# A hybrid pooling and attention trunk: one weight scaling goes from the vector engine to GpSimd, and the vector part of one mixing stage is issued a projection tile later

## Chip, cores and metric

The kernel runs on one core of a Trainium2 chip. The metric is the device time of one execution in microseconds (us), lower is better. Engines are named as the profile names them: PE is the matrix engine, DVE the vector engine, ACT the scalar engine, POOL is GpSimd, SP the engine that issues most of the transfers.

## What is computed

Two layers (DEPTH = 2) of a decoder trunk on 16 meta tokens and 512 tokens with 1024 channels, all in float32:

```python
h = RMSNorm(x)
u_pool, z_pool, c_q, c_kv, k_rope, z_mla, g_pool, g_mla = split(h @ W_in)
y_pool = W_pool_up( PoolMix(u_pool) * silu(z_pool) )
y_mla  = W_mla_up( MLA(c_q, c_kv, k_rope) * silu(z_mla) )
x = x + W_out( sigmoid(g_pool) * y_pool + sigmoid(g_mla) * y_mla )
```

PoolMix works on four groups of 128 channels with windows w = 2, 4, 8 and 16. For each group it takes the mean of the last w tokens (of as many as there are, for the first ones), subtracts the token itself and multiplies the result by a 128x128 matrix. MLA is causal attention with 8 heads; all heads share the rotary part of the key, `k_rope`, which has 32 channels and comes straight out of the input projection.

## The kernel before

Channels lie on the 128 partitions and tokens along the free axis (T = 528 with the meta tokens). Every float32 matmul is done as three (`mm3`, lines 186 to 188): each operand is split into a high part, written by ACT, and a low part, high subtracted from the original, written by DVE, and high x high, high x low and low x high are summed in PSUM. For weights this is done in `wload`: a transfer into a `raw` buffer (three of them, line 115), ACT copies the high part (line 181), DVE subtracts (line 182). `whi` and `wlo` have three buffers each.

The main sequence is a list of projections, `plan`, walked by the generator `stream`: for each 128-wide output tile it loads weights (four chunks of 512 columns ahead), issues the matmuls and then the tile's evacuation out of PSUM (`evac`). The PSUM pool `mm` has four buffers of one bank; layer 0 computes all tokens in two halves of 264 columns and so takes two buffers for a tile, layer 1 computes 512 columns in one for most of them. Other work is put between by hand: `up(name)` walks the stream until that projection is done, then the work that stands after it is issued. Afterwards a list scheduler orders the instructions of each engine, and the engines run in that order, waiting on semaphores.

The order of the projections around the change is: cq0 to cq4, u0, k0, u1, kr, k1, u2, k2, u3, k3, v, zp0, zp1, y0, zp2, y1, zp3, y2, cq5, y3, qr0, qr1. Here:

- `u0` to `u3` are the four pooling groups, evacuated by DVE (line 477), multiplied by the norm factor `rinv`.
- `kr` is the shared rotary key. It isn't split: its weights (`wkr`, 128x256) are multiplied in place by the norm gain in `wload` (line 177) and used as float32 by narrow matmuls (line 416).
- `k0` to `k3` are the heads' keys, evacuated by DVE (line 560).
- `v` (`v_body`) computes values into `vt`: four token tiles and one for the meta tokens, each in a PSUM buffer, read out twice by ACT (line 583, high part) and twice by DVE (line 584, low part). The matmuls for the meta tokens read copies in `pa` (line 592).
- `zp0` to `zp3` are gates: DVE scales (line 486), ACT takes a tanh (line 488), DVE combines (line 489).
- `y0` to `y3` are the 128x128 group matmuls; they read `ys`, the split result of the mixing stages.

A mixing stage m, `mix(m)`, builds the windowed sum of `u` by m + 1 doubling additions on POOL (line 499, results in the `tmp` pool of three buffers), then DVE multiplies by 1/w and subtracts `u` (line 502), corrects the first 16 columns (lines 505 and 506, layer 0 only), and ACT and DVE split the result (lines 277 and 278). In `go`, `mix(2)` stands after `up("u3")` and `mix(3)` after `up("k3")`, so ahead of `v`.

Of the kernel before, what the change touches and what calls it, by code (L numbers as in the profile page):

```python
# [14 lines left out]
ALU = mybir.AluOpType  # L15
# [3 lines left out]
P = 128  # L19
# [3 lines left out]
NM = 16  # L23
T = SEQ + NM
HALF = T // 2
W = 528
WU = 544
# [19 lines left out]
C_MM, C_VBD, C_INVF, C_CNT = 356, 372, 380, 381  # L47
# [25 lines left out]
def trunk(ctx, tc, xT, pos, win, wkr, wqb, wkb, wvb, wgr, wpu, wmu, wout, gains, const, yT):  # L73
    nc = tc.nc
    pe, act, dve, gp, sp = nc.tensor, nc.scalar, nc.vector, nc.gpsimd, nc.sync
# [11 lines left out]
    def nm(s):  # L87
        uid[0] += 1
        return f"{s}_{uid[0]}"

    def slot(tag, dt=F32, bufs=1, w=W):
        return sl.tile([P, w], dt, tag=tag, name=nm(tag), bufs=bufs)

    def tmp(w=W):
        return tp.tile([P, w], F32, tag="tmp", name=nm("tmp"), bufs=3)
# [13 lines left out]
    cst = cp.tile([P, N_CONST], F32, name="cst")  # L109
# [4 lines left out]
    def fetch(src, n, raw, eng):  # L114
        eng.dma_start(raw[:, :n], src)
        return raw

    def rawt():
        return wp.tile([P, 512], F32, tag="raw", name=nm("raw"), bufs=3)
# [22 lines left out]
    def other_loads(made):  # L142
        for k, m in ((2, 0), (4, 1), (6, None)):
            ins = sp.dma_start(xb[:, k:k + 2, :T], xT[:, k:k + 2, :])
            behind(ins, made)
            if m is not None:
                raw = rawt()
                behind(sp.dma_start(raw, win[0, MT_CKV + m, :, 512:1024]), made)
                early.append(raw)
        behind(sp.dma_start(cst, const), made)  # L150
        behind(sp.dma_start(posb[:, :T], pos.partition_broadcast(P)), made)
        dve.tensor_copy(maskw[:, 512 - P:], cst[:, C_MASK:C_MASK + P])
        dve.tensor_copy(identr, ident)
# [17 lines left out]
    def wload(src, n, gain, spare):  # L171
        raw = early.pop(0) if early else fetch(src, n, rawt(), sp)
        loads[0] += 1
        pool, th, tl, nb = (tp, "th", "tl", 2) if loads[0] <= 2 or spare else (wp, "whi", "wlo", 3)
        if gain is not None:
            v = raw[:, :n].rearrange("p (k m) -> p k m", k=8)
            dve.tensor_mul(v, v, gain.unsqueeze(2).to_broadcast([P, 8, n // 8]))
            return raw, None
        hi = pool.tile([P, W if pool is tp else 512], F32R, tag=th, name=nm("whi"), bufs=nb)
        lo = pool.tile([P, W if pool is tp else 512], F32R, tag=tl, name=nm("wlo"), bufs=nb)  # L180
        act.activation(hi[:, :n], raw[:, :n], AF.Copy)  # L181
        dve.tensor_sub(lo[:, :n], raw[:, :n], hi[:, :n].bitcast(F32))  # L182
        return hi, lo
# [10 lines left out]
    def stream():  # L194
# [3 lines left out]
        def load(i):  # L198
            g_, c = flat[i]
            n = min(512, g_.width - c)  # L200
            return wload(g_.src[:, c:c + n], n, g_.gain, g_.spare)
# [37 lines left out]
    def step():  # L239
        c = next(main, None)  # L240
        if c is None:
            flush()
            return False
        clk[0] += c
        while pend and pend[0][0] <= clk[0]:
            pend.pop(0)[1]()
        return True
# [5 lines left out]
    def flush():  # L253
        while pend:
            pend.pop(0)[1]()

    def upto(name):
        while name not in done:
            if not step():
                break  # L260
# [10 lines left out]
    def fill_now(ns):  # L271
        end = clk[0] + ns
        while clk[0] < end and step():
            pass

    def split(hi, lo, src, a, b):
        act.activation(hi[:, a:b], src, AF.Copy)  # L277
        dve.tensor_sub(lo[:, a:b], src, hi[:, a:b].bitcast(F32))  # L278
# [14 lines left out]
    def tables():  # L293
        ang, k = tmp()[:, :T], tmp()[:, :T]
        dve.tensor_scalar(ang, posb[:, :T], float(NM), None, op0=ALU.add)
        dve.tensor_scalar(ang, ang, cst[:, C_INVF:C_INVF + 1], None, op0=ALU.mult)
        dve.tensor_scalar(k, ang, 1.0 / TWO_PI, MAGIC, op0=ALU.mult, op1=ALU.add)
        dve.tensor_scalar(k, k, -MAGIC, None, op0=ALU.add)
        for c in (PI_A, PI_B, PI_C):
            dve.scalar_tensor_tensor(out=ang, in0=k, scalar=-c, in1=ang, op0=ALU.mult, op1=ALU.add)  # L300
        dve.tensor_scalar(ang, ang, 3.1415925, -3.1415925, op0=ALU.min, op1=ALU.max)
        act.activation(tcos, ang, AF.Sin, scale=0.5)
        act.activation(tsin, ang, AF.Sin)
        dve.tensor_mul(tcos, tcos, tcos)
        dve.tensor_scalar(tcos, tcos, -2.0, 1.0, op0=ALU.mult, op1=ALU.add)
# [7 lines left out]
    class Layer:  # L313
# [175 lines left out]
                dve.scalar_tensor_tensor(out=d, in0=t[:, :b - a], scalar=1.0, in1=d, op0=ALU.add, op1=ALU.mult)  # L489
            return ev  # L490

        def mix(self, m):
            u, x0 = self.us[m], self.x0
            s = u
            for e in range(m + 1):
                w = 1 << e
                lo_ = 2 * w if not self.last else NM + 2 * w - 1
                n = tmp(WU)
                gp.tensor_tensor(out=n[:, lo_:WU], in0=s[:, lo_:WU], in1=s[:, lo_ - w:WU - w], op=ALU.add)
                s = n  # L500
            f = tmp()
            dve.scalar_tensor_tensor(out=f[:, x0:T], in0=s[:, NM + x0:WU], scalar=1.0 / (2 << m),
                                     in1=u[:, NM + x0:WU], op0=ALU.mult, op1=ALU.subtract)
            if not self.last:
                dve.tensor_mul(f[:, 0:NM], s[:, NM:2 * NM], cst[:, C_CNT + NM * m:C_CNT + NM * (m + 1)])
                dve.tensor_sub(f[:, 0:NM], f[:, 0:NM], u[:, NM:2 * NM])
            t = "tl" if m % 2 else "th"
            self.ys[m] = (slot(f"u{m}", F32R), tp.tile([P, W], F32R, tag=t, name=nm(t), bufs=2))
            split(*self.ys[m], f[:, x0:T], x0, T)
# [466 lines left out]
        def go(self, nxt):  # L976
            l = self.l
            up = lambda name: upto((l, name))
            if l == 0:
                for k in range(8):  # L980
                    if k in (0, 1, 3, 5):
                        step()
                    self.split_h(k)
                    if k == 0:
                        other_loads(first)
            up("ckv1")
            if l == 0:
                for k in range(8):
                    self.square_x(k)
            self.norm_sums()  # L990
            if l == 0:
                tables()
            up("u1")
            self.mix(0)
            self.mix(1)
            up("u3")
            self.mix(2)
            up("k3")
            self.mix(3)
            up("qr1")  # L1000
            for s, (a, b) in enumerate(FULL):
                a0 = max(a, self.x0)
                self.stat(self.acc[:, a0:b], a0, b, C_CQ, self.acc_last)
            up("qn3")
            self.qk_stats()
            fill_now(2600)
            kq = self.prep(0)
            fill_now(2600)
            due[0] = None
            prev = None  # L1010
            for h in range(H):
                kn_ = self.head(h, kq, prev)
                self.gap()
                if h + 1 < H:
                    kq = self.prep(h + 1)
                self.pv(prev, (2, 3))
                prev = kn_
                self.gap()
            fill_now(1300)
            self.pv(prev, (0, 1))  # L1020
            fill_now(2600)
            if not self.last:
                self.meta_queries()
            self.pv(prev, (2, 3))
            up("gm7")
            flush()
            if not self.last:
                for p in range(4):
                    self.meta_out(p)
            up("o7")  # L1030
            if nxt is not None:
                for k in range(8):
                    nxt.split_h(k)
# [77 lines left out]
```

## Time and profile before

| | |
|---|---|
| timed runs, us | 803.83, 804.71, 804.91 (median 804.71) |
| profiled execution, us | 803.88 |
| its span, us | 802.1 |
| mean granted PE clock over the span | 0.998 |
| PE busy, share of the span | 99% |
| DVE, ACT, POOL busy | 66%, 51%, 25% |
| line 177 on DVE | two executions, 0.42 us each |
| line 499 on POOL (window additions) | 20, of 1.05 to 1.61 us |
| line 502 on DVE | 8, of 0.68 to 0.71 us |

In a timeline row the first number is the start in us from the span's start, the second how long it took (of all of them together, where a row says x2 or more), then engine, source line, operation, the tiles out<-in and their shape. A bracket tells how long the engine had been idle before it and which engine's instruction ended that. In the list of waits a row says who waited for whom, the total in us, how often, and the longest.

### The profile page before, as it was taken

Reading aid. Unit: us, or ns where it says so; the run is one execution under the profiler, and the core shown is the slowest. Engines: PE = TensorE matmul, PEld = TensorE weight load, DVE = VectorE, ACT = ScalarE, POOL = GpSimd, SP = SyncE. Lnnn points to the kernel's source line nnn. Section 1 sums busy time; section 2 is a strip of 40 time slices with the busy share of each in tenths; the row PEclk is TensorE's granted clock in tenths of the full one; section 3 lists DMA queues with packets and bytes.
Section 4 is the critical chain, followed back from the end, with each engine's and each line's share of the span. In section 5 each row is a group of like instructions: output and inputs, shape, how many; then the busy total and the mean of one; then the engine's idle time right before and its main releaser. Section 6 shows DMA issues by size and latency. Waiting matters only on the chain.

```text
span 802.1 us, 14590 instructions
## 1 busy us (share of the span) xinstructions
PE 790.6 (99%) x5321; PEld 712.6 (89%) x5321; DVE 528.1 (66%) x1134; ACT 413.0 (51%) x935; POOL 196.8 (25%) x261
## 2 busy tenths in 40 slices
PE   8999899999999999999999999999999999999998
PEld 8898799999999999999998898877788888887887
DVE  5557867545779897576363469665467888664942
ACT  7455555644565665643354436546445666654421
POOL 1023512201433231133000126112024333410600
PEclk9999999999999999999999999999999999999999
DMA  6242223334223222234652332334253322222273
GB/s 239 67 106 87 67 77 95 106 94 135 82 91 96 73 73 67 77 96 120 187 153 85 76 116 80 93 92 119 80 154 99 100 74 78 75 72 78 92 223 105
DMA packets 51688, 81.80 MB, mean 102 GB/s; under 512 B 8208, under 2 KB 16784, under 8 KB 51616
## 3 DMA queue, kind: packets, MB, share of 16 engines
q1 hardware_dynamic: 51472, 80.61, 34.0%
q8 instruction: 42, 0.69, 0.4%
q14 instruction: 30, 0.25, 0.1%
q10 hardware_dynamic: 144, 0.26, 0.1%
HBM read 74.48 MB, written 4.24 MB: 98 GB/s over the span
## 4 chain that ended last, share of the span: by engine, by line
PE 90%; DMA 4%; DVE 3%; issue 1%; ACT 1%; POOL 1%; SPq 0%; DVEq 0%; ACTq 0%; POOLq 0%
PE mm L186 26%; PE mm L187 26%; PE mm L188 26%; PE mm L799 2%; PE S L187 2%; PE S L188 2%; PE S L186 1%; PE o L805 1%; PE o L804 1%; DMA raw<-win 1%; PE mm L355 1%; PE S L458 1%; DVE wlo L182 1%; DMA xb<-xT 1%; DMA bc<-kdr 1%
## 5 line engine op out<-in xcount | busy, mean ns | idle before, releaser
L186 PE MATMUL mm<-hh,whi 128*128 128x264 f32 (+2 forms) x1096 | 346.6, 318 | 2.5 <-DVE u L477 1.6
L187 PE MATMUL mm<-hl,whi 128*128 128x264 f32 (+2 forms) x1096 | 344.1, 315 | 0.0
L188 PE MATMUL mm<-hh,wlo 128*128 128x264 f32 (+2 forms) x1096 | 342.9, 315 | 0.0
L182 DVE TENSOR_TENSOR wlo<-raw,whi 128x512 fp32r<-128x512 f32 (+2 forms) x251 | 187.3, 750 | 121.0 <-ACT whi L181 117.5
L181 ACT ACTIVATE whi<-raw 128x512 fp32r<-128x512 f32 (+2 forms) x251 | 150.2, 602 | 190.2 <-PE mm L187 125.2
L186 PEld LDWEIGHTS mm<-hh,whi 128*128 128x128 f32 x1096 | 206.1, 189 | 15.9 <-issue 2.4
L187 PEld LDWEIGHTS mm<-hl,whi 128*128 128x128 f32 x1096 | 206.7, 189 | 12.2 <-issue 0.4
L188 PEld LDWEIGHTS mm<-hh,wlo 128*128 128x128 f32 x1096 | 205.7, 188 | 12.6 <-issue 0.4
L536 POOL TENSOR_TENSOR racc<-racc,tmp 128x264 f32<-128x264 f32 (+1 forms) x15 | 14.6, 973 | 186.7 <-ACT tmp L535 186.7
L705 POOL TENSOR_TENSOR tmp<-kp,bc 64x528 f32<-64x528 f32 x16 | 24.6, 1537 | 113.8 <-DMA bc<-kdr 78.6
L777 POOL TENSOR_TENSOR pm<-pa,rs 128x16 f32<-128x16 f32 x32 | 11.6, 361 | 145.4 <-DVE rs L772 145.4
L887 POOL TENSOR_TENSOR tmp<-tmp,xb 128x264 f32<-128x264 f32 (+1 forms) x24 | 27.0, 1149 | 58.5 <-DVE tmp L885 32.3
L733 DVE CUSTOM_DVE_ANT_0 S<-S,maskw,nqs 128x272 f32<-128x272 f32 (+4 forms) x80 | 38.4, 498 | 1.6 <-PE S L188 1.2
L740 ACT ACTIVATE cq<-S,bia 128x400 f32<-128x400 f32 (+2 forms) x48 | 24.6, 516 | 21.6 <-DVE bia L767 11.6
L186 PE MATMUL mm<-u,whi 128*128 128x264 f32 (+1 forms) x108 | 35.3, 327 | 0.0
L188 PE MATMUL mm<-u,wlo 128*128 128x264 f32 (+1 forms) x108 | 34.9, 323 | 0.0
L186 PE MATMUL mm<-cq,whi 128*128 128x264 f32 (+1 forms) x108 | 34.7, 322 | 0.0
L187 PE MATMUL mm<-cq,whi 128*128 128x264 f32 (+1 forms) x108 | 34.7, 322 | 0.0
L188 PE MATMUL mm<-cq,wlo 128*128 128x264 f32 (+1 forms) x108 | 34.6, 322 | 0.0
L278 DVE TENSOR_TENSOR tl<-mm,th 128x512 fp32r<-128x512 f32 (+1 forms) x64 | 29.3, 482 | 6.8 <-ACT th L277 5.8
L779 POOL TENSOR_TENSOR cq<-cq,rs 128x384 f32<-128x384 f32 (+1 forms) x32 | 32.8, 1025 | 0.0
L277 ACT ACTIVATE th<-mm 128x512 fp32r<-128x512 f32 (+1 forms) x64 | 25.4, 433 | 10.6 <-PE mm L799 10.4
(250 smaller groups left out, 1372.2 us busy)
## 6 DMA issues: line engine op xcount, KB each, us to landing
raw<-win SPq DMA_DIRECT2D x143, 256.0 KB, 2.6
raw<-wout SPq DMA_DIRECT2D x32, 256.0 KB, 3.3
bc<-kdr SPq DMA_DIRECT2D x16, 264.0 KB, 3.5
raw<-wpu SPq DMA_DIRECT2D x16, 256.0 KB, 2.7
raw<-wmu SPq DMA_DIRECT2D x16, 256.0 KB, 2.6
raw<-wqb SPq DMA_DIRECT2D x12, 256.0 KB, 2.6
tmp<-xT SPq DMA_DIRECT2D x16, 132.0 KB, 3.2
tmp<-scr SPq DMA_DIRECT2D x7, 256.0 KB, 3.5
```

The source lines that it names most:

```text
L181: act.activation(hi[:, :n], raw[:, :n], AF.Copy)
L182: dve.tensor_sub(lo[:, :n], raw[:, :n], hi[:, :n].bitcast(F32))
L186: pe.matmul(out, wh, xh, start=start, stop=False)
L187: pe.matmul(out, wh, xl, start=False, stop=False)
L188: newest[0] = pe.matmul(out, wl, xh, start=False, stop=stop)
L277: act.activation(hi[:, a:b], src, AF.Copy)
L278: dve.tensor_sub(lo[:, a:b], src, hi[:, a:b].bitcast(F32))
L705: gp.tensor_mul(kf[r0:r0 + 64, :], self.kp[r0:r0 + 64, :], bc[r0:r0 + 64, :])
L733: dve.tensor_tensor_reduce(out=sv, in0=sv, in1=mask, scale=nqs[:, i, h:h + 1], scalar=3e38, op0=ALU.add, op1=ALU.min, accum_out=bia[:, c:c ...
L740: act.activation(pv, sv, AF.Exp, scale=-1.0, bias=bia[:, i:i + 1], accum_out=rs[:, c:c + 1])
L779: gp.tensor_mul(pt[i][:, NM:], pt[i][:, NM:], rs[:, i:i + 1].to_broadcast([P, n - NM]))
L887: gp.tensor_add(t[:, :b - a], t[:, :b - a], self.am[m][:, a:b])
```

## The change

Two edits. In `wload`, the multiplication of the shared key's weights by the gain is issued on POOL instead of DVE. And `mix` is cut in two: `window(m)` holds the additions on POOL, `mix(m, s)` the rest. For m = 0, 1 and 2 they are issued together as before. For m = 3 the additions stay where they were, after `up("k3")`, and the rest is issued after `up("zp0")`. The last addition of m = 3 writes only the columns that are read later, and into the slot `q3` instead of a `tmp` buffer; `q3` is otherwise first used by `qr1`.

In the scheduled program the multiplication stands on POOL ahead of the first window addition in layer 0, and ahead of the last cq4 accumulation (line 536) in layer 1. DVE's instructions of the fourth stage (lines 502, 505, 506 and 278 of before) leave the stretch of line 584 and stand between zp0's line 489 and zp1's line 486. On PE the second group of meta token matmuls of `v` moves a few instructions forward among those of zp0; the rest of the engines' orders is the same but for a few neighbours.

```diff
@@ wload
         if gain is not None:
             v = raw[:, :n].rearrange("p (k m) -> p k m", k=8)
-            dve.tensor_mul(v, v, gain.unsqueeze(2).to_broadcast([P, 8, n // 8]))
+            gp.tensor_mul(v, v, gain.unsqueeze(2).to_broadcast([P, 8, n // 8]))
             return raw, None
@@ class Layer
-        def mix(self, m):
-            u, x0 = self.us[m], self.x0
-            s = u
+        def window(self, m):
+            s = self.us[m]
             for e in range(m + 1):
                 w = 1 << e
                 lo_ = 2 * w if not self.last else NM + 2 * w - 1
-                n = tmp(WU)
-                gp.tensor_tensor(out=n[:, lo_:WU], in0=s[:, lo_:WU], in1=s[:, lo_ - w:WU - w], op=ALU.add)
+                a, n = (lo_, tmp(WU)) if e < m or m < 3 else (NM + self.x0, None)
+                if n is None:
+                    n = slot("q3")
+                    gp.tensor_tensor(out=n[:, a - NM:T], in0=s[:, a:WU], in1=s[:, a - w:WU - w], op=ALU.add)
+                    return n
+                gp.tensor_tensor(out=n[:, a:WU], in0=s[:, a:WU], in1=s[:, a - w:WU - w], op=ALU.add)
                 s = n
+            return s[:, NM:WU]
+
+        def mix(self, m, s=None):
+            u, x0 = self.us[m], self.x0
+            s = self.window(m) if s is None else s
             f = tmp()
-            dve.scalar_tensor_tensor(out=f[:, x0:T], in0=s[:, NM + x0:WU], scalar=1.0 / (2 << m),
+            dve.scalar_tensor_tensor(out=f[:, x0:T], in0=s[:, x0:T], scalar=1.0 / (2 << m),
                                      in1=u[:, NM + x0:WU], op0=ALU.mult, op1=ALU.subtract)
             if not self.last:
-                dve.tensor_mul(f[:, 0:NM], s[:, NM:2 * NM], cst[:, C_CNT + NM * m:C_CNT + NM * (m + 1)])
+                dve.tensor_mul(f[:, 0:NM], s[:, 0:NM], cst[:, C_CNT + NM * m:C_CNT + NM * (m + 1)])
                 dve.tensor_sub(f[:, 0:NM], f[:, 0:NM], u[:, NM:2 * NM])
@@ go
             up("k3")
-            self.mix(3)
+            s = self.window(3)
+            up("zp0")
+            self.mix(3, s)
             up("qr1")
```

## The prediction

> **What bounds the kernel now.** I read the page first, then the waits of PE, then the timeline of each engine around those waits, then windows of the same stretches.
>
> ```profile
> span 802.1 us, 14590 instructions
> ...
> PE 790.6 (99%) x5321; PEld 712.6 (89%) x5321; DVE 528.1 (66%) x1134; ACT 413.0 (51%) x935; POOL 196.8 (25%) x261
> ```
>
> ```profile
> PE mm L186 <- DVE vt L584: 2.8, 1, 2.8
> PE mm L186 <- DVE u L477: 1.6, 1, 1.6
> ```
>
> PE is busy for 790.6 of 802.1 us. An edit on DVE or GpSimd (POOL in the profile) can only pay where PE waits for it, and the list of PE's waits (us in total, times, longest) is led by these two, each happening once in the whole run. Both lie in layer 0, and the two edits touch the neighbourhood of one each. The profiled execution took 803.88 us (span 802.1, so 1.8 around it); the median of the three timed runs is 804.71, 0.83 more, and they spread over 1.08 us. I make the sum against 803.88 and then move it to the median. A change of 0.2%, about what a measurement of this kernel can tell from none, is 1.6 us.
>
> **First edit: the scaling of the shared key's weights (L177) leaves DVE.** Timeline of DVE, ACT, PE and POOL around 60 us:
>
> ```profile
> 58.52 0.48 DVE L526 SCALAR_TENSOR_TENSOR cq<-mm,gn,cq 128x264 fp32r<-128x264 f32 x1
> 60.68 0.43 DVE L177 TENSOR_TENSOR raw<-raw,gn 128x256 f32<-128x256 f32 x1 [1.67 <-DMA raw<-wkr]
> 61.02 0.68 DVE L182 TENSOR_TENSOR wlo<-raw,whi 128x512 fp32r<-128x512 f32 x1
> 61.62 0.77 DVE L477 TENSOR_TENSOR u<-mm,rinv 128x264 f32<-128x264 f32 x2
> ...
> 59.39 1.14 ACT L181 ACTIVATE whi<-raw 128x512 fp32r<-128x512 f32 x2
> ...
> 62.19 0.36 PE L186 MATMUL mm<-hh,whi 128*128 128x264 f32 x1 [1.64 <-DVE u L477]
> ...
> 62.47 1.47 POOL L499 TENSOR_TENSOR tmp<-u 128x542 f32<-128x542 f32 x1 [2.14 <-DVE u L477]
> ...
> 97.96 0.63 ACT L181 ACTIVATE whi<-raw 128x512 fp32r<-128x512 f32 x1 [1.22 <-PE mm L188]
> ```
>
> DVE has nothing to do from 59.00 but stands before L177 until the wkr weights land. Behind it wait a weight split (L182) and the read of the first u tile out of PSUM (L477). PE needs that PSUM buffer for the next u tile. Without L177, L182 waits only for its high part: the first of the two L181 begins at 59.39 and takes 0.63, so it ends at 60.02 instead of L182's present start of 61.02. I take 60.04, an estimate that adds 0.02 for the signal. L182 and L477 keep their spacing, so everything behind moves by 61.02 - 60.04 = 0.98 us: L477 starts at 60.64 and PE at 62.19 - 0.98 = 61.21. Of the 1.64 us wait 0.66 stays. **Gain 0.98.** Bounds: 0, if something else holds DVE as long; 1.64, the whole wait.
>
> On POOL the operation is not in this trace. Nearest rows of the groups by shape, then the timeline where the result is used and the same place in layer 1, then a window of it (columns: stretch, its length, busy us of PE, PEld, DVE, ACT and POOL, granted clock of PE, DMA share, GB/s):
>
> ```profile
> L779 POOL TENSOR_TENSOR pa<-pa,rs 128x256 f32<-128x256 f32 x16 | 10.6, 662 | 0.0
> L536 POOL TENSOR_TENSOR racc<-racc,tmp 128x264 f32<-128x264 f32 x10 | 8.1, 815 | 74.7 <-ACT tmp L535 74.7
> ```
>
> ```profile
> 68.21 1.99 PE L416 MATMUL mm<-xb,raw 128*32 128x264 f32 x32
> ...
> 463.02 1.29 POOL L536 TENSOR_TENSOR racc<-racc,tmp 128x512 f32<-128x512 f32 x1 [4.74 <-ACT tmp L535]
> ...
> 465.19 0.42 DVE L177 TENSOR_TENSOR raw<-raw,gn 128x256 f32<-128x256 f32 x1 [3.00 <-DMA raw<-wkr]
> ...
> 466.98 1.44 POOL L499 TENSOR_TENSOR tmp<-u 128x527 f32<-128x527 f32 x1 [2.67 <-DVE u L477]
> ```
>
> ```profile
> 462.00:512.00 50.00, 50.00 (x356) 44.39 (x355) 37.06 (x74) 27.70 (x61) 22.48 (x25) 1.00 0.31 92
> ```
>
> L779 multiplies in place by a broadcast operand over 128x256, as L177 does, in 0.66 us; L536 takes 0.82. I take 0.7: from about 60.68, when DVE's L177 shows the weights there, to 61.38. Its reader, the shared key's matmul L416, starts at 68.21 (67.23 after the move), so 5.9 us cover it. POOL's next work, the first window addition, can start at 62.47 - 0.98 = 61.49, after L177 is done. One transfer behind it on SP that reuses the same raw buffer gains a wait for POOL, but it waits for L416 already.
>
> In layer 1, L177 stands on POOL ahead of the last L536, which then slips from 463.02 to about 465.9 and ends near 467.2, 0.2 us after the addition L499 could have started. Nothing comes of it, nor of DVE's 3.00 us: PE is busy for 50.00 of the 50 us from 462 on. **Layer 1: 0.**
>
> A rule speaks against moving the multiply. Rows first (timeline, then windows of the same stretch): while POOL added, a 128x512 L182 took 1.51 us instead of 0.68, and a 16-wide L506 1.05.
>
> ```profile
> 90.28 1.51 DVE L182 TENSOR_TENSOR wlo<-raw,whi 128x512 fp32r<-128x512 f32 x1
> 91.72 1.05 DVE L506 TENSOR_TENSOR tmp<-tmp,u 128x16 f32<-128x16 f32 x1
> 93.48 1.21 DVE L278 TENSOR_TENSOR th<-tmp,u 128x528 fp32r<-128x528 f32 x1 [0.71 <-ACT u L277]
> 94.61 1.65 DVE L584 SCALAR_TENSOR_TENSOR vt<-mm,ny,vt 128x256 fp32r<-128x256 f32 x4
> 96.18 0.69 DVE L502 SCALAR_TENSOR_TENSOR tmp<-tmp,u 128x528 f32<-128x528 f32 x1
> ...
> 97.98 0.16 DVE L505 TENSOR_TENSOR tmp<-tmp,cst 128x16 f32<-128x16 f32 x1
> ...
> 99.23 0.17 DVE L506 TENSOR_TENSOR tmp<-tmp,u 128x16 f32<-128x16 f32 x1
> ...
> 100.16 0.71 DVE L278 TENSOR_TENSOR tl<-tmp,u 128x528 fp32r<-128x528 f32 x1 [0.37 <-ACT u L277]
> ...
> 90.16 3.97 POOL L499 TENSOR_TENSOR tmp<-tmp 128x540 f32<-128x540 f32 x3 [1.12 <-DVE tmp L505]
> ...
> 96.41 0.66 PE L186 MATMUL mm<-whi,pa 128*128 128x512 f32 x1 [2.80 <-DVE vt L584]
> ```
>
> ```profile
> 62.20:65.00 2.80, 2.80 (x23) 2.80 (x24) 2.14 (x6) 1.13 (x4) 1.47 (x1) 1.00 0.50 139
> ...
> 93.60:96.40 2.80, 0.00 (x1) 0.03 (x1) 2.80 (x6) 2.21 (x7) 0.53 (x1) 1.00 0.09 33
> 96.40:99.80 3.40, 3.40 (x13) 3.07 (x14) 3.18 (x10) 1.64 (x4) 0.00 (x0) 0.52 0.02 5
> ```
>
> The Trainium skill (SBUF — State Buffer, on the shared port pair) calls this an exclusive lock between GpSimd and a DVE operation with two SBUF inputs: who starts first has it for the whole instruction. The trace agrees in size. By that rule, were L177 first, L182 would wait out its 0.7 us and the gain would be 0.3. I expect DVE first: L182 can start at 60.04 and the weights come at 60.68.
>
> **Second edit: the fourth mixing stage.** PE's other wait, 2.80 us at 96.41, is for the PSUM buffer that the fourth L584 reads out. In DVE's queue that L584 stands behind a split, an L506 and an L278, all stretched by POOL's three additions of 90.16 to 94.13. The last addition now writes slot q3; it is the same addition at the same place. The DVE part that moves (L502, L505, L506 and the low half of its split, with the ACT half between) begins at 96.18, behind the fourth L584. So taking it away frees 0.69 us only after PE has been released. **The 2.80 us stay**, and with them their tail: the windows show the clock at 0.52 for 3.40 us right behind the gap, 3.40 x 0.48 = 1.63 us lost. All links of this chain hang on PE's earlier progress, so the whole stretch only shifts by the 0.98. From 99.80 on PE has no wait that the moved work could have caused: **gain 0**.
>
> What it may cost where it arrives, behind zp0's matmuls:
>
> ```profile
> 106.22 1.35 POOL L607 CAST vb<-tmp 32x128 fp32r<-32x128 f32 x4
> ...
> 107.88 0.43 DVE L489 SCALAR_TENSOR_TENSOR xb<-tmp,xb 128x264 f32<-128x264 f32 x1 [1.45 <-ACT tmp L488]
> ...
> 108.34 0.42 ACT L488 ACTIVATE tmp<-xb 128x264 f32<-128x264 f32 x1 [0.50 <-DVE xb L489]
> ...
> 108.80 0.43 DVE L489 SCALAR_TENSOR_TENSOR xb<-tmp,xb 128x264 f32<-128x264 f32 x1 [0.49 <-ACT tmp L488]
> 109.32 0.69 DVE L182 TENSOR_TENSOR wlo<-raw,whi 128x512 fp32r<-128x512 f32 x1
> 109.93 0.42 DVE L486 SCALAR_TENSOR_TENSOR xb<-mm,rinv 128x264 f32<-128x264 f32 x1
> ...
> 111.31 0.43 DVE L486 SCALAR_TENSOR_TENSOR xb<-mm,rinv 128x264 f32<-128x264 f32 x1
> ...
> 111.83 0.28 PE L186 MATMUL mm<-hh,whi 128*128 128x264 f32 x1
> ```
>
> In these times (all 0.98 earlier after): the new queue is L489, the subtraction, L489, two 16-wide operations, L182, the low half, then L486, which frees zp1's first PSUM buffer. The subtraction (0.69) fits between the L489s, which end at 109.27. The 16-wide ones bring DVE to 109.57, L182 to 110.2. Meanwhile ACT does the high half, 109.62 to 110.27 (0.65, an estimate from L181's 0.63 over 512 columns). The low half takes DVE to about 111.0, and L486 ends near 111.4 instead of 110.35. PE wants that buffer for zp2 at 111.83: 0.4 us of cover left. The second L486 still ends at its 111.74. So 0, with this small cover. In layer 1 the same insertion meets a DVE that is busy 37.06 of 50.00 us: 0.
>
> **Sum.** 803.88 - 0.98 = 802.90 in the profiled execution's terms; against the median 804.71 - 0.98 = 803.73, which I round to 803.7.
>
> **The rivals.**
> - The tail goes, the gap stays. The slow stretch is 3.40 us long, and 1.64 us of waiting at 62.19 drew none (clock 1.00 in the row of 62.20). So the clock may be judged in stretches of this length: the gap of 2.80 us, moved by 0.98, would then fall across two of them, neither idle enough. Gain 0.98 + 1.63 = 2.61: 802.1 against the median. Against: nothing ties such stretches to the kernel's start, so the gap may have fallen badly or well before too. Chance 0.18. The Trainium skill (TensorE: Matmul & The Clock Gate, Part 1) has such a window, about 3.4 us and free-running, which must be idle to halve the clock; the 3.40 us of the trace agree with its length.
> - The second gap goes too. For: DVE is busy all 2.80 us of it. A shift of 0.12 us would let the split at 90.28 go ahead of the addition at 90.16, and the queue behind would be shorter. Against: the same instructions stand ahead of the fourth L584. Gain 0.98 + 2.80 + 1.63 = 5.41: 799.3. Chance 0.18.
> - L177 was not the gate (gain 0), or POOL begins it before L182 and holds L182 up for its 0.7 us, as an addition held the one at 90.28 (gain 0.98 - 0.7 = 0.3): 804.4 to 804.7. The first needs a second hold on DVE of the same length, the second the weights 0.64 us earlier. Chance 0.08.
> - Slower: the inserted work makes zp1's evacuation late. Its operations in series (rows of 96.18 to 100.16) are 0.69 + 0.16 + 0.17 + 0.65 + 0.71 = 2.4 us. If nothing overlaps (POOL's L607 late for the subtraction's buffer, ACT late with the high half), L486 ends at 110.35 + 2.4 = 112.75 and PE, due at 111.83, waits 0.92 us plus 0.15 for the signal (the fourth L584 ends at 96.26, PE starts at 96.41). With a slow-clock tail of 1.63 that is 2.7 - 0.98 = +1.7: 806.4. It decides from 0.4 us of delay on, and is over 0.2% only with all of it and the tail. For: the cover is thin. Against: POOL's L607 ends at 107.57, before the subtraction can start. Chance 0.14.
>
> **How the numbers follow.** Forecast 0.42. Within 0.2% are the forecast and the third rival, 0.50; faster by over 0.2% the first two, 0.36; slower 0.14. The range reaches down to the second rival, 799.0, and up to 805.6, which covers the third with the spread of the runs upward (0.9); only the slower case is outside. The forecast's own range is 802.6 to 804.9.
>
> **What would show it.** Right: PE's wait for L477 near 0.66 us, L177 on POOL at about 0.7 us, the wait for L584 still about 2.8 us, and no wait of PE at the start of zp2. Wrong: the L584 wait below 2 us, the first wait unchanged, or a new wait of PE for L486.

## The result, and the profile after

| | before | after |
|---|---|---|
| runs of one comparison, median us | 804.81 (803.32 to 807.46, 20 runs) | 802.7 (800.62 to 805.44, 20 runs) |
| ratio, 95% interval | | 0.9972 [0.9963, 0.998] |
| profiled execution / span, us | 803.88 / 802.1 | 802.87 / 801.1 |
| mean granted clock in it | 0.998 | 1.0 |

Faster by 2.1 us, and by the whole interval faster than the kernel before: twice the 0.98 us forecast, in the forecast's direction and inside its range. Line numbers: `wload` is unmoved; the window additions (L499) are now L502, the last one L500; L502 of before is L510, and what follows is 8 higher as well (L506 is L514, L536 is L544, L584 is L592).

The page of after, its first rows:

```profile
span 801.1 us, 14595 instructions
...
PE 791.3 (99%) x5321; PEld 713.3 (89%) x5321; DVE 528.3 (66%) x1132; ACT 413.6 (52%) x935; POOL 199.2 (25%) x263
```

Nothing shows here but that POOL has two operations more and DVE two fewer. The list of PE's waits of after says where to look (us in total, times, longest):

```profile
PE mm L186 <- DVE vt L592: 2.8, 1, 2.8
...
PE mm L186 <- DVE u L477: 0.8, 1, 0.8
```

The wait for the first u tile fell from 1.6 to 0.8 us, the wait for vt is the same 2.8. The first of these can't be read as the gain by itself: before, run again below, waits only 0.8 us there too. The timeline of after around the first (DVE, ACT, PE, then POOL):

```profile
61.37 0.83 DVE L182 TENSOR_TENSOR wlo<-raw,whi 128x512 fp32r<-128x512 f32 x1 [1.04 <-ACT whi L181]
62.12 0.76 DVE L477 TENSOR_TENSOR u<-mm,rinv 128x264 f32<-128x264 f32 x2
...
60.72 1.14 ACT L181 ACTIVATE whi<-raw 128x512 fp32r<-128x512 f32 x2
...
62.69 0.36 PE L186 MATMUL mm<-hh,whi 128*128 128x264 f32 x1 [0.82 <-DVE u L477]
...
60.16 1.49 POOL L544 TENSOR_TENSOR racc<-racc,tmp 128x264 f32<-128x264 f32 x2 [3.75 <-ACT tmp L543]
62.16 0.62 POOL L177 TENSOR_TENSOR raw<-raw,gn 128x256 f32<-128x256 f32 x1 [0.51 <-DMA raw<-wkr]
62.96 1.47 POOL L502 TENSOR_TENSOR tmp<-u 128x542 f32<-128x542 f32 x1 [0.18 <-DVE u L477]
```

In this execution everything here begins later than in before's (the pair of L181 at 60.72 instead of 59.39), so compare from L181 on: L182 now waits for ACT's L181 and not behind a wait for a transfer, and PE restarts (its first matmul behind the wait) 62.69 - 60.72 = 1.97 us after L181's start, where it took 62.19 - 59.39 = 2.80. That is 0.83 us less. L177 takes 0.62 us on POOL, after DVE's L182 has begun.

The second place, DVE, PE and POOL of after:

```profile
90.79 1.51 DVE L182 TENSOR_TENSOR wlo<-raw,whi 128x512 fp32r<-128x512 f32 x1
92.22 1.05 DVE L514 TENSOR_TENSOR tmp<-tmp,u 128x16 f32<-128x16 f32 x1
93.98 1.21 DVE L278 TENSOR_TENSOR th<-tmp,u 128x528 fp32r<-128x528 f32 x1 [0.71 <-ACT u L277]
95.11 2.82 DVE L592 SCALAR_TENSOR_TENSOR vt<-mm,ny,vt 128x256 fp32r<-128x256 f32 x7
...
96.91 0.47 PE L186 MATMUL mm<-whi,pa 128*128 128x512 f32 x1 [2.81 <-DVE vt L592]
...
90.67 2.58 POOL L502 TENSOR_TENSOR tmp<-tmp 128x540 f32<-128x540 f32 x2 [1.12 <-DVE tmp L513]
93.32 1.31 POOL L500 TENSOR_TENSOR q<-tmp 128x528 f32<-128x528 f32 x1
```

The same three operations with the same durations to the hundredth (1.51, 1.05, 1.21) as before, beside the same additions. What differs is behind the gap: windows of after, two of 3.4 us around PE's restart and two longer ones (length, busy us of PE, PEld, DVE, ACT and POOL, granted clock, DMA share, GB/s).

```profile
93.50:96.90 3.40, 0.59 (x3) 0.18 (x2) 2.92 (x6) 2.82 (x8) 1.13 (x1) 1.00 0.22 74
96.90:100.30 3.40, 3.39 (x25) 3.26 (x26) 2.39 (x7) 1.34 (x3) 0.00 (x0) 1.00 0.02 6
...
105.00:112.00 7.00, 7.00 (x60) 7.00 (x59) 5.22 (x13) 4.98 (x11) 1.35 (x5) 1.00 0.21 64
...
462.00:512.00 50.00, 50.00 (x352) 44.18 (x352) 38.64 (x74) 27.78 (x61) 23.46 (x26) 1.00 0.28 85
```

The clock stays at 1.00 behind the gap, where before's profile had 0.52 for 3.40 us: no tail in this execution. PE is busy throughout from 105 to 112, where the moved DVE part arrives, and from 462 to 512, where layer 1 has its L177.

So after's profile has PE's restart 0.83 us earlier behind L181, the gap as it was, no tail. Is the missing tail the change's doing, and what would remove the gap? The experiments ask that.

### The profile page after: what moved, and what is told of

Same layout as the page of the kernel before. It is cut to its first block, busy times and chain, and to the rows that moved or that the text cites. A ratio compares the mean times of both kernels' runs of the same rounds, so it can differ in the third digit from the quotient of the medians.

```text
span 801.1 us, 14595 instructions
## 1 busy us (share of the span) xinstructions
PE 791.3 (99%) x5321; PEld 713.3 (89%) x5321; DVE 528.3 (66%) x1132; ACT 413.6 (52%) x935; POOL 199.2 (25%) x263
## 4 chain that ended last, share of the span: by engine, by line
PE 90%; DVE 3%; DMA 3%; issue 1%; ACT 1%; POOL 1%; SPq 0%; ACTq 0%; DVEq 0%; POOLq 0%
PE mm L186 26%; PE mm L188 26%; PE mm L187 26%; PE mm L807 2%; DMA raw<-win 2%; PE S L187 2%; PE S L188 2%; PE S L186 2%; PE o L813 1%; PE o L812 1%; PE mm L355 1%; DVE wlo L182 1%; PE S L458 1%; DMA bc<-kdr 1%; PE mm L416 0%
## 5 line engine op out<-in xcount | busy, mean ns | idle before, releaser
L182 DVE TENSOR_TENSOR wlo<-raw,whi 128x512 fp32r<-128x512 f32 (+2 forms) x251 | 186.6, 747 | 121.9 <-ACT whi L181 115.2
L181 ACT ACTIVATE whi<-raw 128x512 fp32r<-128x512 f32 (+2 forms) x251 | 150.2, 602 | 186.8 <-PE mm L187 136.7
L544 POOL TENSOR_TENSOR racc<-racc,tmp 128x264 f32<-128x264 f32 (+1 forms) x15 | 14.9, 996 | 182.4 <-ACT tmp L543 158.5
```

## The experiments

Theories, as the expectations use the letters: **A**, only the first edit makes a lasting gain, by what DVE stood in front of L177, and the rest of the 2.1 us is how often the slow clock follows the gap. **B**, the second edit brings that rest, by making the slow clock rarer. **C**, the two edits pay only together. Beside them stands the question what makes the gap: the additions, as the prediction has it, or something else. Each ratio is against the runs of the kernel before in the same comparison.

### Each edit alone, and both kernels again

The first edit alone is before with one line changed:

```diff
-            dve.tensor_mul(v, v, gain.unsqueeze(2).to_broadcast([P, 8, n // 8]))
+            gp.tensor_mul(v, v, gain.unsqueeze(2).to_broadcast([P, 8, n // 8]))
```

> Only the first edit: L177 on POOL, the fourth mixing stage as before. Theory A (the first edit is the whole lasting gain, about 1 us; the rest of the 2.1 us is how often the slow clock follows the 2.8 us gap): 1.0 us under before in the mean, PE's wait for the first u tile 0.6 to 0.9 us, the wait for L584 2.8 us, and the slow clock in some executions only. Theory B (the second edit brings the missing 1.1 us, by making the slow clock rarer): also 1.0 us under before, but the slow clock about as often as before. Theory C (the two edits only work together): less than 0.5 us.

Measured: 801.51 us (12 runs), ratio 0.9989 [0.9979, 0.9998], against 802.52 (35 runs) of before. Its timeline, DVE, ACT, PE, POOL:

```profile
60.03 0.84 DVE L182 TENSOR_TENSOR wlo<-raw,whi 128x512 fp32r<-128x512 f32 x1 [1.04 <-ACT whi L181]
60.79 0.76 DVE L477 TENSOR_TENSOR u<-mm,rinv 128x264 f32<-128x264 f32 x2
...
59.37 1.14 ACT L181 ACTIVATE whi<-raw 128x512 fp32r<-128x512 f32 x2
...
61.35 0.36 PE L186 MATMUL mm<-hh,whi 128*128 128x264 f32 x1 [0.45 <-DVE u L477]
...
58.82 1.50 POOL L536 TENSOR_TENSOR racc<-racc,tmp 128x264 f32<-128x264 f32 x2 [3.75 <-ACT tmp L535]
```

This execution begins the stretch at the same moment as before's profile did (L181 at 59.37 and 59.39), so the absolute times can be compared: L182 starts at 60.03 (predicted 60.04), L477 at 60.79 instead of 61.62, PE at 61.35 instead of 62.19. It gains 0.84 us, not 0.98, because L182 takes 0.84 here and 0.68 in before. Here it begins while POOL's pair of L536 (58.82 to 60.32) is still running, in before it began after it. PE's wait is 0.45 us, under the 0.6 to 0.9 expected, because PE comes to it later than in before's profile: 61.35 - 0.45 - 59.37 = 1.53 us after L181's start, where it was 62.19 - 1.64 - 59.39 = 1.16. The wait for vt is 2.8 us.

The second edit alone is after with `dve` in that line:

> Only the second edit: L177 stays on DVE. Theory A: 0 +- 0.4 us against before, both of PE's waits as before (1.6 and 2.8 us). Theory B: 1.1 us under before, and the granted clock is 1.000 in more executions than before. Theory C: less than 0.5 us.

Measured: 802.07 (11 runs), ratio 0.9994 [0.9986, 1.0003]; the wait for vt 2.8 us, the first wait 1.1 where 1.6 was expected. It can't be told from before.

After again:

> The changed kernel once more, on the same chip as its two halves. Theory A: 1 to 2 us under before, the mean clock below 1.000 in about half of the executions, as in the 20 of the first comparison. Theory B: 2.1 us, and e1 and e2 add up to it.

Measured: 800.79 (12 runs), ratio 0.998 [0.9972, 0.9989]; the wait for vt 2.8 us.

Before again, as a measure of what a comparison can tell:

> The kernel before against itself, for its spread and for how often its clock is below 1.000. Theory A: about as often as in the changed kernel (half), and a difference of 0 +- 0.4 us. Theory B: clearly more often than in the changed kernel.

Measured: 802.07 (11 runs), ratio 0.9993 [0.9982, 1.0004]. The same kernel comes out 0.45 us under its own median, so half a microsecond is not a difference here. The two edits alone, 0.9989 and 0.9994, multiply to 0.9983, beside 0.998 for both: nothing needs theory C.

Before's second profile also shows how PE's first wait varies (DVE, ACT, PE):

```profile
59.65 0.42 DVE L177 TENSOR_TENSOR raw<-raw,gn 128x256 f32<-128x256 f32 x1 [1.77 <-DMA raw<-wkr]
...
58.26 1.21 ACT L181 ACTIVATE whi<-raw 128x512 fp32r<-128x512 f32 x2
...
61.17 0.36 PE L186 MATMUL mm<-hh,whi 128*128 128x264 f32 x1 [0.82 <-DVE u L477]
```

With L177 on DVE, PE waits only 0.82 us here, because it comes to the wait 61.17 - 0.82 - 58.26 = 2.09 us after L181's start. From L181 to PE's restart it is 2.91 us, no shorter than the 2.80 of the first profile. So the gain of the first edit is read from that stretch and not from the wait.

Executions that list a mean clock of 0.999 or more are taken here as those without the tail: the three profiles with one (before, after again, the second edit alone) list 0.997 or 0.998, the others 1.0. In this comparison they are 7 of 35 and 5 of 11 for before, 5 of 12 for the first edit alone, 4 of 11 for the second alone, 6 of 12 for both. The second edit alone has no more of them than before again, and the same median (802.07), not 1.1 us less: nothing speaks for B.

The profiles of after again and before again also answer for the tail. Windows of after again, then of before again, each with the 3.4 us up to the restart or the slow stretch and the 3.4 us behind:

```profile
92.40:95.80 3.40, 0.87 (x4) 0.77 (x5) 3.40 (x8) 2.28 (x6) 0.24 (x1) 1.00 0.01 2
95.80:99.20 3.40, 3.40 (x18) 3.40 (x17) 1.51 (x5) 0.99 (x2) 0.00 (x0) 0.51 0.09 24
```

```profile
91.90:95.30 3.40, 0.69 (x3) 0.21 (x2) 2.86 (x6) 2.82 (x8) 1.19 (x1) 1.00 0.19 72
95.30:98.70 3.40, 3.26 (x22) 2.83 (x23) 3.15 (x10) 2.06 (x5) 0.00 (x0) 1.00 0.02 5
```

After has the tail in this execution (0.51 for 3.4 us) and before has none: the reverse of the first two profiles, from the same two kernels. The tail comes in some executions of either kernel. It isn't something that the second edit takes away.

### The additions of the fourth stage moved too

In the next kernel both halves of the stage stand behind zp0's matmuls:

```diff
-            s = self.window(3)
             up("zp0")
-            self.mix(3, s)
+            self.mix(3)
```

> The changed kernel, but the additions of the fourth mixing stage move along with its DVE part, behind zp0's matmuls, so that no addition of GpSimd runs beside the split, the 16-wide operation and the subtraction that stand ahead of the fourth read of vt. Theory (the wait of 2.8 us is made by those three, stretched by GpSimd's three additions): they take 0.68 + 0.17 + 0.71 again instead of 1.51 + 1.05 + 1.21 us, so the wait falls by about 2.2 to about 0.6 us, and without a gap of that length no stretch at half clock follows it: nearly every execution at full clock, the median 2.2 + 0.9 = 3.1 us under the changed kernel's (ratio to before 0.994). Rival (something else holds the fourth read of vt, such as the additions of the third stage or the order of DVE's queue): the wait stays over 2 us and the time within 0.8 us of the changed kernel's. Second rival (the whole stage is too long for its new place): the wait goes, but PE waits for the evacuation at zp1 or zp2, and the time is within 1 us of the changed kernel's or over it.

Measured: 799.37 us (799.29 to 800.08, 5 runs), ratio 0.9938 [0.9926, 0.995]; before 804.2 (17 runs). That is 3.4 us under after in the same comparison (802.77). The split ahead of the three operations in before, then DVE and PE of this kernel:

```profile
88.01 1.58 DVE L182 TENSOR_TENSOR wlo<-raw,whi 128x512 fp32r<-128x512 f32 x1
```

```profile
87.50 0.68 DVE L182 TENSOR_TENSOR wlo<-raw,whi 128x512 fp32r<-128x512 f32 x1
...
88.87 0.68 DVE L182 TENSOR_TENSOR wlo<-raw,whi 128x512 fp32r<-128x512 f32 x1
89.47 0.17 DVE L514 TENSOR_TENSOR tmp<-tmp,u 128x16 f32<-128x16 f32 x1
90.80 0.71 DVE L278 TENSOR_TENSOR th<-tmp,u 128x528 fp32r<-128x528 f32 x1 [1.16 <-ACT u L277]
91.42 2.83 DVE L592 SCALAR_TENSOR_TENSOR vt<-mm,ny,vt 128x256 fp32r<-128x256 f32 x7
...
93.23 0.47 PE L186 MATMUL mm<-whi,pa 128*128 128x512 f32 x1 [0.36 <-DVE vt L592]
```

The three operations take 0.68 + 0.17 + 0.71 = 1.56 us instead of 1.51 + 1.05 + 1.21 = 3.77: 2.21 less, and the wait falls from 2.80 to 0.36, by 2.44. So GpSimd's additions made the gap. They stretched one operation more than the prediction counted: the split before these three took 1.58 us beside the first addition and takes 0.68 here. The Trainium skill (SBUF — State Buffer, on the shared port pair) says that a GpSimd operation that reads SBUF and a DVE operation with two SBUF inputs exclude each other for a whole instruction; the trace agrees for these three, each stretched beside the additions (a 16-wide operation sixfold, 0.17 to 1.05) and at its own time without them. Nothing shows up where the stage now stands: PE is busy throughout from 96 to 114 us. The gap is 2.44 of the 3.4 us. The rest fits the tail, which by their clocks nine of after's twelve executions had and none of these five: after's three without it have a mean of 801.78, this kernel 799.51, which is 2.27 us less.

After again in this comparison:

> The changed kernel once more, beside the same runs of the kernel before. If what it gained over the forecast was lasting: a ratio to before near 0.9975, 2 us. If only the first edit pays: 0.9988, 1 us. Wait for vt 2.8 us either way.

Measured: 802.77 (12 runs), ratio 0.9983 [0.997, 0.9996]; the wait for vt 2.8 us.

The same with the additions behind v and the DVE part behind zp1 (`up("v")`, `s = self.window(3)`, `up("zp1")`, `self.mix(3, s)`):

> The changed kernel with both halves of the fourth stage later: the additions behind v's matmuls, the DVE part behind those of zp1. Theory of the gap: the additions still come after the split, the 16-wide operation and the subtraction ahead of the fourth read of vt, so the wait is as short as with the whole stage behind zp0 (0.6 us), and the time is within 0.5 us of that kernel's. If the place of the additions inside v's matmuls still meets the reads of vt, the wait stays over 1.5 us. If the DVE part at zp1 collides with the evacuation there, PE waits for L486 and the time is 0.5 to 2 us over that kernel's.

Measured: 799.75 (799.48 to 801.0, 5 runs), ratio 0.9943 [0.9931, 0.9956]; the wait for vt 0.4 us. Within 0.4 us of its sibling: so for the gap it matters where the additions stand, and not where the DVE part does.

### The first edit without the gap

With the gap and its tail away, the first edit can be priced alone: the kernel with the whole stage behind zp0, and L177 back on DVE.

> As the kernel with the whole fourth stage behind zp0's matmuls, but with the scaling of the shared key's weights back on DVE. It prices the first edit alone with the long gap out of the way. Theory (the first edit removes only what DVE stood before L177, 0.6 to 1.0 us): 0.6 to 1.0 us over its twin, PE's wait for the first u tile near 1 us or over, where the twin has under 0.8. Rival (the first edit's gain comes through the clock, by moving the gap against the windows of the clock gate): no gap, so no difference, within 0.3 us of its twin.

Measured: 800.81 (799.79 to 801.15, 5 runs), 1.44 us over its twin (799.37). Its DVE, ACT and PE, then the twin's:

```profile
61.11 0.43 DVE L177 TENSOR_TENSOR raw<-raw,gn 128x256 f32<-128x256 f32 x1 [1.69 <-DMA raw<-wkr]
61.45 0.69 DVE L182 TENSOR_TENSOR wlo<-raw,whi 128x512 fp32r<-128x512 f32 x1
...
59.80 1.15 ACT L181 ACTIVATE whi<-raw 128x512 fp32r<-128x512 f32 x2
...
62.63 0.36 PE L186 MATMUL mm<-hh,whi 128*128 128x264 f32 x1 [1.67 <-DVE u L477]
```

```profile
60.37 0.83 DVE L182 TENSOR_TENSOR wlo<-raw,whi 128x512 fp32r<-128x512 f32 x1 [1.04 <-ACT whi L181]
...
59.72 1.14 ACT L181 ACTIVATE whi<-raw 128x512 fp32r<-128x512 f32 x2
...
61.69 0.36 PE L186 MATMUL mm<-hh,whi 128*128 128x264 f32 x1 [0.82 <-DVE u L477]
```

From L181 to PE's restart 2.83 us with L177 on DVE, 1.97 with it on POOL: 0.86. Both kernels were run again, as 1.44 was more than that:

> The kernel with both edits and the whole fourth stage late, again. 0.85 us under its twin below if the traces' difference (the first u tile read 1.40 us after the high halves begin, 2.25 in the twin) is the whole of the first edit; 1.1 to 1.4 us if the earlier runs' difference of the means and the medians was no accident. Nearly every execution at full clock, as no gap of 2.8 us is left.

> The same with the scaling of the shared key's weights on DVE, again: 0.85 us over the twin above, or 1.1 to 1.4; full clock as there.

Measured: 799.7 (799.1 to 800.56) and 799.97 (799.73 to 800.99), 6 runs each, ratios 0.995 [0.9933, 0.9967] and 0.9954 [0.9938, 0.9971]. Over both comparisons the means of the two kernels are 799.66 and 800.38 (11 runs each): 0.72 us. The two comparisons give 1.14 and 0.37 for it, so five or six runs scatter too much to price an edit of this size. In all twelve profiles of kernels with the tables before u1 the stretch from L181 to PE is 1.97 or 1.98 us with L177 on POOL (seven profiles) and 2.80 to 2.92 with it on DVE (five). By the traces the first edit is worth 0.8 to 0.9 us, by these runs about 0.7, and it needs no gap and no tail for that.

### The wait that is left

0.8 us of the first wait stay, behind ACT's L181. The last kernel is the one with the whole stage behind zp0 (L177 on POOL), and moves the rotary tables, which ACT and DVE work on ahead of that split, behind u1:

```diff
-            if l == 0:
-                tables()
             up("u1")
+            if l == 0:
+                tables()
             self.mix(0)
```

> The kernel with the whole fourth stage behind zp0's matmuls, and the rotary tables (their table load, two activations and two DVE operations) issued after u1 instead of before it, so that ACT and DVE have some 3 us less to do ahead of the weight splits that the first u tile stands behind. If those splits wait for ACT's own queue, PE's first wait (0.8 us) goes nearly whole, and the time is 0.5 to 0.8 us under that of the kernel with the tables before u1. If they wait for what PE or a transfer delivers, or the tables now delay the first two mixing stages, nothing is gained, or up to 1 us is lost.

Measured: 801.66 (801.11 to 802.31, 12 runs), ratio 0.9971 [0.9961, 0.9982], 2.0 us over its sibling of the same comparison (799.7). PE's waits of this kernel:

```profile
PE mm L186 <- DVE u L477: 1.9, 3, 1.0
...
PE mm L186 <- DVE vt L592: 1.0, 1, 1.0
```

2.9 us in place of 0.8 + 0.4: 1.7 more, most of the 2.0. On DVE the table steps (L300, 0.69 us each) now stand between the reads of u. A miss, and outside what was allowed for (1 us). The wait it leaves for vt, 1.0 us, brought no slow stretch in 12 executions.

## Why the prediction was right, and where not

**First edit, 0.98: right in mechanism and place, 0.14 too large.** L182 started at 60.03 (60.04 said), and PE's restart came 0.84 us earlier. The step that missed is "L182 and L477 keep their spacing": L182 grew from 0.68 to 0.84, a term that the prediction had at nothing. Most likely that comes of beginning beside POOL's accumulation (L536): L182 takes 0.83 or 0.84 us in all seven profiles where it does and 0.68 or 0.69 in the five where it doesn't, but no run took the accumulation away. The wait left is 0.3 to 0.8 us (0.66 said). The 1.64 it was worked out from was one execution's: in the profiles with L177 on DVE the wait is 0.8 to 1.7 us, by when PE comes to it. L177 on POOL: 0.62 us (0.7 said), started behind L182, hidden. In layer 1 it stands at 463.90, ahead of the accumulation, and PE has no wait there: 0, as said.

```profile
463.90 0.62 POOL L177 TENSOR_TENSOR raw<-raw,gn 128x256 f32<-128x256 f32 x1 [6.58 <-DVE u L477]
464.48 1.30 POOL L544 TENSOR_TENSOR racc<-racc,tmp 128x512 f32<-128x512 f32 x1
```

**Second edit, 0: right.** Alone it can't be told from before, the gap is 2.8 us in every kernel that leaves the additions in place, and the reason given, the additions stretching three operations ahead of the fourth L584, is what the kernel without them shows, with a fourth operation that it didn't count. Where the DVE part arrives it went as worked out, in after's timeline:

```profile
107.18 0.70 DVE L510 SCALAR_TENSOR_TENSOR tmp<-q,u 128x528 f32<-128x528 f32 x1
...
109.23 0.71 DVE L278 TENSOR_TENSOR tl<-tmp,u 128x528 fp32r<-128x528 f32 x1
109.86 0.86 DVE L486 SCALAR_TENSOR_TENSOR xb<-mm,rinv 128x264 f32<-128x264 f32 x2
```

The subtraction lies between the two L489, the low half ahead of L486, and the pair of L486 comes late without holding PE up. The slower rival did not happen.

**The tail, "stays": the wrong step.** It was read from one profile as a property of the kernel. Each run lists its mean clock, and the kernel before has runs at 0.999 or more, without the tail, in 21 of 80 (in the later comparisons, the only ones that list it), after in 19 of 44. The rival that let the tail go described after's profiled execution exactly, but not the kernel. Beside the same runs of before, at 0.999 and more, after gained 801.14 - 799.94 = 1.20 us (7 and 6 runs) in one comparison and 803.09 - 801.78 = 1.31 (4 and 3) in the other.

**What stays open.** After's three comparisons give 0.9972, 0.998 and 0.9983, that is 2.25, 1.6 and 1.4 us, where the traces explain 0.84. The rest is between 0.5 and 1.4 us, so the mechanism accounts for the direction and for 0.84 of the 2.1; that 802.7 still lies inside even the forecast's own range, at its lower end, is in part luck. A part of the rest could be the tail's frequency; by the shares above (0.43 - 0.26) x 1.5 us, an estimate from the means of before with and without it (802.68 and 801.14), 0.26 us. Whether that frequency differs at all is not settled: in the two comparisons that list it for both kernels it is 9 of 24 for after and 16 of 63 for before, a lead that chance alone would give about once in five times, and before itself had 7 of 35 and 5 of 11 side by side. Among the executions without the tail of the first of these two, the first edit alone was 801.14 - 800.40 = 0.74 us under before (7 and 5 runs), near its 0.84; after was 0.46 further down, of the size by which a kernel differed from itself (0.45).

## What to carry to other kernels

When PE waits for a DVE operation that stands in a queue, look not only at what is queued ahead of it but at what GpSimd runs beside those operations: here moving the DVE work of a stage gained nothing, and moving GpSimd's additions of the same stage another 3.4 us, the tail included. An in-order engine that stands before a transfer holds everything behind it; give such an operation to an engine whose next work is far off, and price it by the start of the operation behind it. Don't count a slow-clock stretch of one profile as the kernel's: read the clock of every run.

## What was not expected of the hardware

A gap of the same 2.8 us was followed by a half-clock stretch of 3.4 us in some executions and not in others, of the same kernel. In two profiles with a tail PE was busy for 0.60 us (before, 93.00 to 96.40) and 0.87 us (after again) of the 3.4 us just ahead of it; after and before again had 3.4 us with only 0.59 and 0.69 busy and no tail. A fixed grid of such stretches that lies differently in each execution could explain both, but no run shows the grid. All 39 runs of the four kernels without that gap (no wait of PE over 1.7 us) list 0.999 or more. The Trainium skill (TensorE: Matmul & The Clock Gate, Part 1) asks for an idle window of about 3.4 us; here the 3.4 us ahead of a slow stretch had PE busy for a quarter of them (0.87).
